# Modulation rows in a fixed order: all products, then three row turns, then the transpositions

## The chip, the cores and the metric

The kernel runs on one core of a Trainium2 chip. The metric is the device time of one execution in microseconds (us). The core has five engines that run beside each other, each with its own queue in order: TensorE (PE, with weight loads shown apart as PEld), VectorE (DVE), ScalarE (ACT), GpSimd (POOL) and SyncE (SP), which issues most transfers. An engine waits for another only at a semaphore, and whatever stands behind a waiting instruction in the same queue waits with it.

## The reference

One block of a diffusion transformer over 2048 tokens of width 1024, with 256 context tokens. What matters here is its beginning:

```python
mod_x = (jax.nn.silu(c) @ w_mod[layer] + b_mod[layer])[:, None, :]
mod_c = jax.nn.silu(c_ctx) @ w_mod[layer] + b_mod[layer]
sh1, sc1, g1, sh2, sc2, g2 = jnp.split(mod_x, 6, axis=-1)
csh1, csc1, cg1, csh2, csc2, cg2 = jnp.split(mod_c, 6, axis=-1)
hx = _rmsnorm(x, norm1_g[layer]) * (1.0 + sc1) + sh1
hc = _rmsnorm(ctx, norm1_g[layer]) * (1.0 + csc1) + csh1
feats_x = _mixer_features(hx, w_in[layer], lb, (rows, cols))
```

Nothing of the token mixers can start before the shift `sh1` and the scale `sc1` are known: a vector of 1024 inputs times a 1024 x 2048 part of `w_mod`, for two vectors (`c` and `c_ctx`). Behind this come two mixers with four heads each, the output projection, and a convolutional feed-forward network.

## The kernel before

The 2048 tokens are worked in four groups of 512; the last group (3) comes first. `heads` is the driver of the first two thirds of the time. It begins with the weights of head 0 (`items`: `w_z`, `w_q`, `w_vg`, each weight turned into pairs of 16-bit numbers by a cast on ACT, line 703 or 760, and a subtraction on DVE, line 704 or 761, with a few sums of quarters between them, lines 548 to 557), and with the modulation.

The 2048 columns of the modulation that are needed first are worked as four quarters of 512 columns, in the order 2, 3, 0, 1. Each quarter takes these steps:

- `mod_first` (line 292): eight PE products of 512 columns, each with one of eight 128-row pieces of the quarter's weights (`wm`), into four squares of 32 rows of one PSUM bank, `mod_ps`. Two banks of this kind (tag `sc`) are there.
- `mod_rows`: a copy of that bank to SBUF, the row `modrow` (line 256 on ACT, or 258 on DVE for quarter 0); four small PE products that turn the row into columns, the "row turn" (`modt_ps`, line 263); and one DVE addition of the bias into `modT` (line 266).

Quarter 2 is done early, with both kernels alike. Then `norm_rows` normalises the first 512 tokens (`x3`, whose eight pieces of 128 x 512 are shown as `hc` and `x`): eight squares with sums, all on ACT (line 398), a sum on DVE (402), six small POOL instructions for the reciprocal root (`rstd`, lines 71 to 76), and the scaling of the eight pieces by it, half on DVE (409) and half on ACT (407). `modulation` forms from `modT` the scale `modu` and the sums `modq` (DVE, lines 355 to 369), which go through one PE product (`allsum`) and five tiny DVE instructions to a power of two, `p2s`. `first_blocks` transposes the normalised tokens on PE (`tp`, line 416), applies scale and shift (`ftmp`, lines 460 on ACT and 458 on DVE), and casts to pairs of 16-bit numbers (`hx`, lines 435 on ACT and 436 on DVE) with `p2s`; then the first product of a head can run.

The order in each engine's queue is set by a scheduler that builds the program in the order of the code and moves instructions by its own estimates; `issue_after(x)` in the code keeps an instruction behind `x` in that order. It is no wait on the chip. Waits come from the data alone, buffers that are used again among them.

Of the kernel before, what the change touches and what calls it, by code (L numbers as in the profile page):

```python
# [9 lines left out]
F32 = mybir.dt.float32  # L10
# [4 lines left out]
AF = mybir.ActivationFunctionType  # L15
# [3 lines left out]
P = 128  # L19
# [13 lines left out]
KL = 3  # L33
# [21 lines left out]
class Kern:  # L55
# [191 lines left out]


    def mod_rows(self, rows, nr, j4):


        nc = self.nc
        if nr == 2:
            rs = self.mp.tile([P, 512], F32, tag="Kl", bufs=KL, name="modrow")
            if j4:
                nc.scalar.copy(rs, rows)
            else:
                nc.vector.tensor_copy(rs, rows)
            rows = rs
        ps = self.ps("tu", [P, 4, 2], "modt_ps")  # L260
        for j in range(4):
            sel = self.sel if nr == 2 else self.ones
            self.moded = nc.tensor.matmul(ps[:, j, :nr], rows[:, j * P:(j + 1) * P], sel, start=True, stop=True, skip_group_check=True)
        o = self.modT[:, :nr, 4 * j4:4 * j4 + 4].rearrange("p d j -> p j d")
        bm = view(self.sv, V_BM + 4 * j4, [[1, 4], [0, nr]])
        nc.vector.tensor_tensor(o, ps[:, :, :nr], bm, ALU.add)
# [19 lines left out]
    def mod_first(self, j4):  # L286

        nc = self.nc
        ps = self.ps("sc", [P, 512], "mod_ps")
        for k, w in enumerate(self.wm[j4]):  # L290
            q = k % 4 * B
            nc.tensor.matmul(ps[q:q + B], self.silb[:, k], w, start=k < 4, stop=k >= 4, skip_group_check=True)
        return ps
# [91 lines left out]

    def norm_rows(self, g, xn, behind=None):

# [5 lines left out]
        for i in range(nt):  # L393
            for h in range(2):
                on_act = True
                with self.tc.issue_after(behind[on_act].ins) if behind else nullcontext():
# [5 lines left out]
        nc.vector.tensor_tensor(ssq[:, :nt], sq[:, :nt, 0], sq[:, :nt, 1], ALU.add)  # L402
        r = self.rstd(self.mp, ssq[:, :nt], nt, D)
        for i in range(nt):
            for h in range(2):
                if h:
                    nc.scalar.activation(xn[i][h], xn[i][h], AF.Copy, scale=r[:, i:i + 1])
                else:
                    nc.vector.tensor_scalar(xn[i][h], xn[i][h], r[:, i:i + 1], None, ALU.mult)
        return xn  # L410
# [8 lines left out]
    def first_blocks(self, g, xn, places, bank, plain=False):  # L419
# [26 lines left out]
        for k0 in (0, 2):  # L446
            f = [places[k0 + r]() for r in range(2)]
            units = [(slice(k0, k0 + 2), f)] if len(f[0]) == len(f[1]) == 1 else [(slice(k0 + i, k0 + i + 1), []) for i in range(2)]
            for i in range(2):
                k = k0 + i  # L450
                at = [(v[0][:, i] if len(v) == 1 else v[i])[:, :2 * n] for v in f]
                for r in range(2):
                    kk = k + 4 * r
                    with self.tc.issue_after(self.moded.ins) if plain and k + r > 1 else nullcontext():
                        tp = self.transposed(xn, kk, bank)
# [241 lines left out]
    def pair_blocks(self, raws, W, s, neg, eng):  # L697

        nc = self.nc

        def emit(m, v):
            sc = neg if m == 3 else s
            nc.scalar.activation(W[m][:, 0], v, AF.Copy, scale=sc)  # L703
            nc.vector.scalar_tensor_tensor(W[m][:, 1], v, sc, W[m][:, 0], ALU.mult, ALU.subtract)  # L704
        blocks = [r[:, 4 * c:4 * c + 4] for r in raws for c in range(2)]
        yield from self.left_blocks(blocks, emit, eng.tensor_tensor)
# [332 lines left out]
    def heads(self):  # L1039
# [6 lines left out]
        self.small_vectors()  # L1046
        self.mod_rows(r2, 2, 2)
        self.lower_bounds()
        for _, comp in items[4:]:
            comp()  # L1050
        self.norm_rows(NG - 1, self.x3)
        self.mod_rows(self.mod_first(3), 2, 3)
        rows = [self.mod_first(j) for j in range(2)]
        for j in range(2):
            self.mod_rows(rows[j], 2, j)
        place = [self.gate_tile() for _ in range(4)]
# [941 lines left out]
```

## Time and profile before

| | |
|---|---|
| median of 3 runs | 2597.32 us (2592.52 to 2599.94) |
| profiled execution | 2600.73 us, span 2599.0 us |
| mean granted TensorE clock | 0.989 |
| PE busy | 2500.6 us (96% of the span) |
| DVE, ACT, POOL busy | 1895.5, 1351.0, 385.4 us |
| DMA | 402.36 MB, 155 GB/s in the mean |

The span is the time from the first to the last instruction of the profiled execution; 1.7 us of its device time lie around it. In a row of the timeline stand the start, the time to the end of the last of the instructions that it merges, the engine, the line, what is written and read, the number, and in brackets how long the engine had been idle and what ended that. Of the matrix products of this kind of 32-bit data each one shows as two instructions in the trace.

### The profile page before, as it was taken

What the parts mean: (1) busy time and instruction counts of PE and PEld (TensorE: products, weight loads), DVE (VectorE), ACT (ScalarE), POOL (GpSimd) and SP (SyncE); (2) the same over time, 40 slices, a digit from 0 to 9 for tenths busy, and PEclk for the clock granted to TensorE, in tenths of its full rate; (3) what the DMA queues carried; (4) which work ended last, traced back from release to release, by engine and by line L of the source; (5) the groups of instructions that cost most, each with busy time, mean ns of one, the idle gap of its engine ahead of it and who ended that gap; (6) DMA issues with size and microseconds to landing.
All of it is one profiled execution on the core that took longest, in us unless ns stands there. A gap on an engine that the chain in (4) does not pass through costs nothing.

```text
span 2599.0 us, 56245 instructions
## 1 busy us (share of the span) xinstructions
PE 2500.6 (96%) x22761; PEld 1647.9 (63%) x22761; DVE 1895.5 (73%) x4304; ACT 1351.0 (52%) x2879; POOL 385.4 (15%) x377
## 2 busy tenths in 40 slices
PE   5899998999999999999999999999999999999998
PEld 3788887889899999895544444444444444444443
DVE  6798586776878777785659777888888887223766
ACT  7886466564655454553647555556655554211221
POOL 1100000000000000001232343434443442000000
PEclk8999999999999999999999999999999999999999
DMA  8334342442558667794421332233233326544552
GB/s 308 113 135 132 119 147 83 139 152 67 180 164 284 214 214 253 246 332 148 167 82 48 124 112 99 101 111 114 102 106 110 122 90 246 197 173 154 211 213 83
DMA packets 144789, 402.36 MB, mean 155 GB/s; under 512 B 16144, under 2 KB 16372, under 8 KB 139921
## 3 DMA queue, kind: packets, MB, share of 16 engines
q1 hardware_dynamic: 134976, 381.81, 42.0%
q10 hardware_dynamic: 9248, 16.79, 2.0%
q8 instruction: 178, 2.92, 0.5%
q14 instruction: 83, 0.67, 0.1%
q0 software_dynamic: 304, 0.17, 0.0%
HBM read 302.77 MB, written 95.94 MB: 153 GB/s over the span
## 4 chain that ended last, share of the span: by engine, by line
PE 72%; DVE 11%; issue 6%; ACT 5%; DMA 5%; POOL 1%; SPq 0%; ACTq 0%; DVEq 0%; POOLq 0%
PE pa L101 8%; PE pa L102 8%; PE pa L103 8%; PE pd L102 5%; PE pd L101 5%; PE pd L103 5%; PE pc L101 3%; PE pc L103 3%; PE pc L102 3%; PE pb L101 2%; PE pb L102 2%; PE pb L103 2%; DMA raw<-in_w_in_dram 2%; PE opp L101 2%; PE opp L103 2%
## 5 line engine op out<-in xcount | busy, mean ns | idle before, releaser
L101 PE MATMUL pa<-feat,w 128*128 128x512 f16 x704 | 265.5, 382 | 7.2 <-DVE tb L638 4.1
L103 PE MATMUL pa<-feat,w 128*128 128x512 f16 x704 | 268.5, 382 | 1.3 <-DVE w L704 1.3
L102 PE MATMUL pa<-feat,w 128*128 128x512 f16 x704 | 268.4, 381 | 0.0
L102 PE MATMUL pd<-wd,actl 128*128 128x512 f16 x616 | 233.3, 379 | 0.0
L103 PE MATMUL pd<-wd,actl 128*128 128x512 f16 x616 | 233.3, 379 | 0.0
L101 PE MATMUL pd<-wd,actl 128*128 128x512 f16 x616 | 232.6, 379 | 0.0
L103 PEld LDWEIGHTS <-w 128*128 128x128 f16 x1232 | 120.8, 98 | 150.3 <-DVE w L704 4.3
L102 PEld LDWEIGHTS <-w 128*128 128x128 f16 x1232 | 120.8, 98 | 149.4 <-issue 10.9
L101 PEld LDWEIGHTS <-w 128*128 128x128 f16 x1232 | 120.8, 98 | 142.0 <-issue 3.1
L102 PEld LDWEIGHTS <-hx 128*128 128x128 f16 x1824 | 178.7, 98 | 6.3 <-issue 4.2
L101 PEld LDWEIGHTS <-hx 128*128 128x128 f16 x1824 | 179.0, 98 | 2.4 <-DVE qs L690 0.3
L103 PEld LDWEIGHTS <-hx 128*128 128x128 f16 x1824 | 178.8, 98 | 1.3 <-issue 0.4
L1474 POOL TENSOR_TENSOR ssq<-ssq 128x1 f32<-128x1 f32 x16 | 6.7, 417 | 1136.1 <-ACT junk L1469 1136.1
L1719 ACT ACTIVATE st<-act,modT 128x512 f16<-128x512 f32 x154 | 107.3, 717 | 113.0 <-DVE act L1709 61.5
L1720 DVE SCALAR_TENSOR_TENSOR st<-act,modT,st 128x512 f16<-128x512 f32 x154 | 143.9, 967 | 29.0 <-ACT st L1719 28.6
L101 PE MATMUL pa<-w_vg,hx 128*128 128x128 f16 x800 | 141.6, 219 | 2.0 <-ACT ct L604 1.2
L102 PE MATMUL pa<-w_vg,hx 128*128 128x128 f16 x800 | 141.6, 219 | 0.3 <-DVE w_vg L704 0.3
L103 PE MATMUL pa<-w_vg,hx 128*128 128x128 f16 x800 | 141.5, 219 | 0.0
L103 PE MATMUL pc<-feat,w 128*128 128x512 f16 x352 | 133.3, 379 | 2.0 <-DVE w L704 2.0
L101 PE MATMUL pc<-feat,w 128*128 128x512 f16 x352 | 133.4, 379 | 0.3 <-ACT tb L604 0.3
L102 PE MATMUL pc<-feat,w 128*128 128x512 f16 x352 | 133.4, 379 | 0.0
L704 DVE SCALAR_TENSOR_TENSOR w<-wur,p2s,w 128x512 f16<-128x512 f32 x132 | 122.8, 938 | 6.0 <-ACT w L703 6.0
(553 smaller groups left out, 7305.1 us busy)
## 6 DMA issues: line engine op xcount, KB each, us to landing
hx<-hxd SPq DMA_DIRECT2D x212, 512.0 KB, 5.2
actd<-st SPq DMA_DIRECT2D x154, 256.0 KB, 2.0
actl<-actd SPq DMA_DIRECT2D x28, 1024.0 KB, 5.2
wur<-in_w_up_dram SPq DMA_DIRECT2D x44, 512.0 KB, 3.6
raw<-in_w_in_dram SPq DMA_DIRECT2D x36, 512.0 KB, 4.6
wm<-in_w_mod_dram SPq DMA_DIRECT2D x64, 256.0 KB, 4.2
hxd<-hx SPq DMA_DIRECT2D x28, 512.0 KB, 4.1
wdb<-in_w_down_dram SPq DMA_DIRECT2D x44, 256.0 KB, 3.8
```

Of the source, the lines that this page charges most:

```text
L101: mm(ps, lhs(0), rhs(0), start=start, stop=False, skip_group_check=True)
L102: mm(ps, lhs(0), rhs(1), start=False, stop=False, skip_group_check=True)
L103: mm(ps, lhs(1), rhs(0), start=False, stop=stop, skip_group_check=True)
L704: nc.vector.scalar_tensor_tensor(W[m][:, 1], v, sc, W[m][:, 0], ALU.mult, ALU.subtract)
L1474: nc.gpsimd.tensor_tensor(ssq[:, 0:1], ssq[:, 0:1], ssq[:, 1:2], ALU.add)
L1719: nc.scalar.activation(p[:, 0], v, AF.Copy, scale=s)
L1720: nc.vector.scalar_tensor_tensor(p[:, 1], v, s, p[:, 0], ALU.mult, ALU.subtract)
```

## The change

In `heads`, quarters 3, 0 and 1 are no longer worked one after another behind the norm. Their 24 products stand in one piece ahead of all row turns, the three row turns follow (each kept behind the last product), and the first transpositions, which had no such bound, are kept behind the last product too. `norm_rows` gets two arguments for the first tokens: its squares are kept behind the last cast of `w_vg`, and are shared, the even pieces on DVE and the odd ones on ACT; and between the squares and the scaling stand the products and row copies of quarters 3 (ACT) and 0 (DVE), with the scaling on each engine kept behind that engine's copy. The copy is a function of its own now, `mod_copy`.

```diff
--- before.py
+++ after.py
@@ -246,17 +246,15 @@
         nc.vector.tensor_scalar(self.omlb, self.lb, -1.0, 1.0, ALU.mult, ALU.add)
 
 
+    def mod_copy(self, rows, eng):
+
+        rs = self.mp.tile([P, 512], F32, tag="Kl", bufs=KL, name="modrow")
+        return rs, eng(rs, rows)
+
     def mod_rows(self, rows, nr, j4):
 
 
         nc = self.nc
-        if nr == 2:
-            rs = self.mp.tile([P, 512], F32, tag="Kl", bufs=KL, name="modrow")
-            if j4:
-                nc.scalar.copy(rs, rows)
-            else:
-                nc.vector.tensor_copy(rs, rows)
-            rows = rs
         ps = self.ps("tu", [P, 4, 2], "modt_ps")
         for j in range(4):
             sel = self.sel if nr == 2 else self.ones
@@ -289,7 +287,7 @@
         ps = self.ps("sc", [P, 512], "mod_ps")
         for k, w in enumerate(self.wm[j4]):
             q = k % 4 * B
-            nc.tensor.matmul(ps[q:q + B], self.silb[:, k], w, start=k < 4, stop=k >= 4, skip_group_check=True)
+            self.rowed = nc.tensor.matmul(ps[q:q + B], self.silb[:, k], w, start=k < 4, stop=k >= 4, skip_group_check=True)
         return ps
 
     def mod_later(self, j4):
@@ -383,7 +381,7 @@
                 self.nc.sync.dma_start(x[h], src[i * P:(i + 1) * P, h * 512:h * 512 + 512])
         return xn
 
-    def norm_rows(self, g, xn, behind=None):
+    def norm_rows(self, g, xn, behind=None, between=None):
 
         nc = self.nc
         nt = len(xn)
@@ -392,7 +390,7 @@
         sq = self.mp.tile([P, 4, 2], F32, tag="sq8", bufs=2, name="sq8")
         for i in range(nt):
             for h in range(2):
-                on_act = True
+                on_act = not between or h
                 with self.tc.issue_after(behind[on_act].ins) if behind else nullcontext():
                     if on_act:
                         nc.scalar.activation(self.junk, xn[i][h], AF.Square, accum_out=sq[:, i, h:h + 1])
@@ -401,12 +399,14 @@
         ssq = self.mp.tile([P, 4], F32, tag="ssq", bufs=2, name="ssq")
         nc.vector.tensor_tensor(ssq[:, :nt], sq[:, :nt, 0], sq[:, :nt, 1], ALU.add)
         r = self.rstd(self.mp, ssq[:, :nt], nt, D)
+        after = between() if between else None
         for i in range(nt):
             for h in range(2):
-                if h:
-                    nc.scalar.activation(xn[i][h], xn[i][h], AF.Copy, scale=r[:, i:i + 1])
-                else:
-                    nc.vector.tensor_scalar(xn[i][h], xn[i][h], r[:, i:i + 1], None, ALU.mult)
+                with self.tc.issue_after(after[h].ins) if after else nullcontext():
+                    if h:
+                        nc.scalar.activation(xn[i][h], xn[i][h], AF.Copy, scale=r[:, i:i + 1])
+                    else:
+                        nc.vector.tensor_scalar(xn[i][h], xn[i][h], r[:, i:i + 1], None, ALU.mult)
         return xn
 
     def transposed(self, xn, k, bank):
@@ -451,7 +451,7 @@
                 at = [(v[0][:, i] if len(v) == 1 else v[i])[:, :2 * n] for v in f]
                 for r in range(2):
                     kk = k + 4 * r
-                    with self.tc.issue_after(self.moded.ins) if plain and k + r > 1 else nullcontext():
+                    with self.tc.issue_after((self.moded if k + r > 1 else self.rowed).ins) if plain else nullcontext():
                         tp = self.transposed(xn, kk, bank)
                     ka, kb = (v[:, which, kk:kk + 1] for v in (A, B))
                     if r and (g is None or plain and i):
@@ -700,8 +700,8 @@
 
         def emit(m, v):
             sc = neg if m == 3 else s
-            nc.scalar.activation(W[m][:, 0], v, AF.Copy, scale=sc)
-            nc.vector.scalar_tensor_tensor(W[m][:, 1], v, sc, W[m][:, 0], ALU.mult, ALU.subtract)
+            cast = nc.scalar.activation(W[m][:, 0], v, AF.Copy, scale=sc)
+            self.laid = nc.vector.scalar_tensor_tensor(W[m][:, 1], v, sc, W[m][:, 0], ALU.mult, ALU.subtract), cast
         blocks = [r[:, 4 * c:4 * c + 4] for r in raws for c in range(2)]
         yield from self.left_blocks(blocks, emit, eng.tensor_tensor)
 
@@ -1044,15 +1044,21 @@
             comp()
         r2 = self.mod_first(2)
         self.small_vectors()
-        self.mod_rows(r2, 2, 2)
+        self.mod_rows(self.mod_copy(r2, nc.scalar.copy)[0], 2, 2)
         self.lower_bounds()
         for _, comp in items[4:]:
             comp()
-        self.norm_rows(NG - 1, self.x3)
-        self.mod_rows(self.mod_first(3), 2, 3)
-        rows = [self.mod_first(j) for j in range(2)]
-        for j in range(2):
-            self.mod_rows(rows[j], 2, j)
+        rows = {}
+
+        def columns():
+            for j, eng in ((3, nc.scalar.copy), (0, nc.vector.tensor_copy)):
+                rows[j] = self.mod_copy(self.mod_first(j), eng)
+            return rows[0][1], rows[3][1]
+        self.norm_rows(NG - 1, self.x3, self.laid, columns)
+        rows[1] = self.mod_copy(self.mod_first(1), nc.scalar.copy)
+        with self.tc.issue_after(self.rowed.ins):
+            for j in (3, 0, 1):
+                self.mod_rows(rows[j][0], 2, j)
         place = [self.gate_tile() for _ in range(4)]
         xc = self.load_rows(None, place)
         self.mod1 = self.modulation(self.ep, pool, view(self.sv, V_N1, [[0, 2], [1, 8]]), self.modT[:, :, 8:16],
```

What the scheduler makes of it differs in the first part of the program, to about the 115th microsecond of the trace of before, and in one short stretch a tenth of the way through PE's queue; behind and between these the queues of all engines hold the same instructions in the same order. SP's queue differs in one swap of two stores of `hx`; POOL's is the same. Names end in buffer numbers below. In the rows of ACT and DVE, the engine or DMA queue whose semaphore an instruction waits for stands after "waits".

PE's queue behind quarter 2, before; `mod_ps_423` is quarter 3, `mod_ps_440` quarter 0, `hc` with a number a piece of the first tokens:

```order
L292 MATMUL mod_ps_423<-wm_213,silb_175 32x512 x2
L416 MATMUL tp_509<-ident_160,hc0_153 128x128
L416 MATMUL tp_515<-ident_160,hc1_154 128x128
L416 MATMUL tp_521<-ident_160,hc0_153 128x128
L292 MATMUL mod_ps_423<-wm_215,silb_175 32x512 x2
L416 MATMUL tp_509<-ident_160,hc2_155 128x128
L416 MATMUL tp_521<-ident_160,hc2_155 128x128
L416 MATMUL tp_515<-ident_160,hc3_156 128x128
L416 MATMUL tp_509<-ident_160,hc4_157 128x128
L416 MATMUL tp_521<-ident_160,hc4_157 128x128
L416 MATMUL tp_515<-ident_160,hc5_158 128x128
L416 MATMUL tp_509<-ident_160,hc6_159 128x128
```

The fourth pair of products of quarter 3 stood behind three transpositions of normalised tokens, and quarter 0, with quarter 1 after it, behind eight more. The same place now, with `mod_ps_445` for quarter 1:

```order
L290 MATMUL mod_ps_445<-wm_225,silb_175 32x512 x2
L290 MATMUL mod_ps_445<-wm_227,silb_175 32x512 x2
L290 MATMUL mod_ps_445<-wm_229,silb_175 32x512 x2
L290 MATMUL mod_ps_445<-wm_231,silb_175 32x512 x2
L261 MATMUL modt_ps_456<-sel_177,modrow_424 128x2 x4
L261 MATMUL modt_ps_462<-sel_177,modrow_435 128x2 x4
L261 MATMUL modt_ps_468<-sel_177,modrow_454 128x2 x4
L416 MATMUL tp_509<-ident_160,hc0_153 128x128
L416 MATMUL tp_515<-ident_160,hc1_154 128x128
L416 MATMUL tp_521<-ident_160,hc0_153 128x128
L416 MATMUL tp_509<-ident_160,hc2_155 128x128
L416 MATMUL tp_521<-ident_160,hc2_155 128x128
```

All products and all row turns stand ahead of the first transposition.

ACT's queue around the squares (`junk`, `sq8`) of the first tokens, before:

```order
L398 ACTIVATE junk_394,sq8_395<-hc2_155 128x512 [waits DMAHW6_49,Activation_49]
L398 ACTIVATE junk_394,sq8_395<-hc3_156 128x512 [waits DMAHW7_49,Activation_49]
L398 ACTIVATE junk_394,sq8_395<-hc4_157 128x512 [waits DMAHW0_49,Activation_49]
L398 ACTIVATE junk_394,sq8_395<-hc5_158 128x512 [waits DMAHW1_49,Activation_49]
L398 ACTIVATE junk_394,sq8_395<-hc6_159 128x512 [waits DMAHW2_49,Activation_49]
L398 ACTIVATE junk_394,sq8_395<-x3_200 128x512 [waits DMAHW3_49,Activation_49]
L760 ACTIVATE w_q_329<-raw_194,p2s_337 128x512 [waits DVE_49]
L760 ACTIVATE w_q_330<-raw_194,p2s_337 128x512
L703 ACTIVATE w_vg_351<-raw_196,p2s_366 128x512 [waits DVE_49]
L703 ACTIVATE w_vg_352<-raw_196,p2s_366 128x512
L703 ACTIVATE w_vg_354<-raw_198,neg_372 128x512 [waits DVE_49]
L407 ACTIVATE hc1_154<-hc1_154,rs_y_407 128x512 [waits Pool_49]
```

The squares stood ahead of the casts of `w_q` and `w_vg`, and waited for ACT's own earlier square and their transfer alone. The same place now:

```order
L703 ACTIVATE w_vg_357<-raw_198,p2s_366 128x512 [waits DVE_49]
L703 ACTIVATE w_vg_356<-raw_196,p2s_366 128x512 [waits DVE_49]
L703 ACTIVATE w_vg_353<-raw_196,p2s_366 128x512 [waits DVE_49]
L396 ACTIVATE junk_394,sq8_395<-hc1_154 128x512 [waits DMAHW5_49,DVE_49]
L396 ACTIVATE junk_394,sq8_395<-hc3_156 128x512 [waits DMAHW7_49,DVE_49]
L396 ACTIVATE junk_394,sq8_395<-hc5_158 128x512 [waits DMAHW1_49,DVE_49]
L396 ACTIVATE junk_394,sq8_395<-x3_200 128x512 [waits DMAHW3_49,DVE_49]
L252 COPY modrow_454<-mod_ps_445 128x512 [waits DMAHW0_49,DMASW0_49,PE_49]
L407 ACTIVATE hc1_154<-hc1_154,rs_y_407 128x512 [waits Activation_49,Pool_49]
L407 ACTIVATE hc3_156<-hc3_156,rs_y_407 128x512 [waits Activation_49]
L407 ACTIVATE hc5_158<-hc5_158,rs_y_407 128x512 [waits Activation_49]
L407 ACTIVATE x3_200<-x3_200,rs_y_407 128x512 [waits Activation_49]
```

All casts stand ahead of the squares, only four squares are left, each waits for DVE, and the row copy of quarter 1 (`modrow_454`) stands between squares and scaling.

DVE's queue from the sum of the squares (`ssq`) to the scaling, before:

```order
L402 TENSOR_TENSOR ssq_404<-sq8_395 128x4 [waits Activation_49]
L116 TENSOR_SCALAR p2s_366<-p2i_365 128x1 [waits DVE_49]
L716 COPY dq_374<-p2i_365 128x1
L713 TENSOR_SCALAR neg_372<-p2s_366 128x1 [waits DVE_49]
L761 SCALAR_TENSOR_TENSOR w_q_329<-raw_194,p2s_337,w_q_329 128x512 [waits DMAHW1_49,Activation_49]
L761 SCALAR_TENSOR_TENSOR w_q_330<-raw_194,p2s_337,w_q_330 128x512 [waits Activation_49]
L704 SCALAR_TENSOR_TENSOR w_vg_351<-raw_196,p2s_366,w_vg_351 128x512 [waits DMAHW2_49,Activation_49]
L704 SCALAR_TENSOR_TENSOR w_vg_352<-raw_196,p2s_366,w_vg_352 128x512 [waits Activation_49]
L409 TENSOR_SCALAR hc0_153<-hc0_153,rs_y_407 128x512 [waits DMAHW4_49,Pool_49]
L409 TENSOR_SCALAR hc2_155<-hc2_155,rs_y_407 128x512 [waits DMAHW6_49]
L409 TENSOR_SCALAR hc4_157<-hc4_157,rs_y_407 128x512 [waits DMAHW0_49]
L409 TENSOR_SCALAR hc6_159<-hc6_159,rs_y_407 128x512 [waits DMAHW2_49]
```

The scaling stood ahead of most of the casts of `w_vg`. The same place now, behind the last cast:

```order
L704 SCALAR_TENSOR_TENSOR w_vg_353<-raw_196,p2s_366,w_vg_353 128x512 [waits Activation_49]
L398 SCALAR_TENSOR_TENSOR junk_394,sq8_395<-hc0_153 128x512 [waits DMAHW4_49]
L252 COPY modrow_435<-mod_ps_426 128x512 [waits DMASW3_49,DMASW4_49,DMASW2_49,DMASW5_49,DMASW1_49,PE_49]
L398 SCALAR_TENSOR_TENSOR junk_394,sq8_395<-hc2_155 128x512 [waits DMAHW6_49,Activation_49]
L398 SCALAR_TENSOR_TENSOR junk_394,sq8_395<-hc4_157 128x512 [waits DMAHW0_49,Activation_49]
L398 SCALAR_TENSOR_TENSOR junk_394,sq8_395<-hc6_159 128x512 [waits DMAHW2_49,Activation_49]
L400 TENSOR_TENSOR ssq_404<-sq8_395 128x4 [waits Activation_49]
L409 TENSOR_SCALAR hc0_153<-hc0_153,rs_y_407 128x512 [waits Pool_49]
L409 TENSOR_SCALAR hc2_155<-hc2_155,rs_y_407 128x512
L409 TENSOR_SCALAR hc4_157<-hc4_157,rs_y_407 128x512
L409 TENSOR_SCALAR hc6_159<-hc6_159,rs_y_407 128x512
L264 TENSOR_TENSOR modT_170<-modt_ps_456,sv_168 128x4x2 [waits PE_49]
```

Each of DVE's squares but the first waits for ACT, since all eight write the one tile `junk_394`; the row copy of quarter 0 (`modrow_435`) stands behind the first, and the additions into `modT` behind the scaling.

## The prediction

> **What bounds the kernel now.** I first read where PE, the engine with the most work, is not busy. The stretches of the span show for each the length, then PE's, PEld's, DVE's, ACT's and POOL's busy time, the granted clock, the DMA share and GB/s:
>
> ```profile
> 0.00:50.00 50.00, 28.06 (x141) 14.08 (x142) 26.63 (x83) 34.28 (x61) 8.26 (x21) 0.83 0.94 357
> ...
> 50.00:100.00 50.00, 40.25 (x449) 32.85 (x447) 41.30 (x83) 44.01 (x95) 4.88 (x12) 0.93 0.39 148
> ...
> 100.00:150.00 50.00, 43.19 (x576) 36.78 (x576) 44.68 (x122) 40.32 (x100) 3.17 (x6) 0.90 0.39 143
> ...
> 300.00:400.00 100.00, 98.02 (x1704) 87.87 (x1697) 79.10 (x209) 62.54 (x150) 0.00 (x0) 1.00 0.42 140
> ```
>
> PE is idle for 21.9 us of the first 50, 9.8 of the next, 6.8 of the next, and from then on it is nearly full. A change at the start is worth what it moves of the moment at which PE gets its work; once moved, PE carries the lead through. PE's own rows between 20 and 52 us show that moment:
>
> ```profile
> 24.91 3.55 PE L292 MATMUL mod_ps<-wm,silb 128*32 128x512 f32 x12
> ...
> 33.72 0.92 PE L416 MATMUL tp<-ident,hc 128*128 128x128 f32 x3 [5.26 <-DVE hc L409]
> ...
> 34.57 1.92 PE L292 MATMUL mod_ps<-wm,silb 128*32 128x512 f32 x4
> ...
> 44.10 1.91 PE L292 MATMUL mod_ps<-wm,silb 128*32 128x512 f32 x12
> ...
> 46.69 1.05 PE L263 MATMUL modt_ps<-sel,modrow 128*128 128x2 f32 x8 [0.69 <-ACT modrow L256]
> ...
> 48.71 0.35 PE L124 MATMUL allsum<-modq,ones 128*128 128x1 f32 x2
> ```
>
> PE waited 5.26 us for the first normalised piece, with products of quarter 3 queued behind it; the last products of quarter 1 ended at 46.0, the last row turn at 47.7, and the sum that gives `p2s` ran at 48.7. So before, the products were late because they stood behind the norm. Were their weights there? SP's row and the DMA row (one issue near 26.7 us; its last number is the time to landing):
>
> ```profile
> 17.11 9.95 SPq L277 DMA_DIRECT2D wm<-in_w_mod_dram  x12
> ...
> wm<-in_w_mod_dram SPq DMA_DIRECT2D x1, 512.0 KB, 10.6
> ```
>
> The last of the twelve pieces landed at about 26.7 + 10.6 = 37.3 us. This is the floor for the products, 8.7 us ahead of 46.0.
>
> **The change part by part.** The transfers do not move: SP's queue is the same up to a swap of two stores. PE has the same instructions. What must be followed is the norm, which now starts behind the casts. ACT and DVE before:
>
> ```profile
> 20.82 0.56 ACT L256 COPY modrow<-mod_ps 128x512 f32<-128x512 f32 x1
> ...
> 28.70 0.63 ACT L398 ACTIVATE junk<-x 128x512 f16<-128x512 f32 x1
> ...
> 29.23 0.19 ACT L398 ACTIVATION_READ_ACCUMULATOR junk<-x 128x1 f32 x1
> ...
> 29.32 1.32 ACT L760 ACTIVATE w_q<-raw,p2s 128x512 f16<-128x512 f32 x2
> ...
> 50.28 1.32 ACT L435 ACTIVATE hx<-ftmp,p2s 128x512 f16<-128x512 f32 x2
> ```
>
> ```profile
> 25.09 0.14 DVE L116 TENSOR_SCALAR p2s<-p2i 128x1 int32<-128x1 int32 x1
> ...
> 29.45 0.16 DVE L402 TENSOR_TENSOR ssq<-sq 128x4 f32<-128x4 f32 x1 [3.71 <-ACT junk L398]
> ...
> 30.06 1.41 DVE L761 SCALAR_TENSOR_TENSOR w_q<-raw,p2s,w_q 128x512 f16<-128x512 f32 x2 [0.20 <-ACT w_q L760]
> ...
> 31.39 1.41 DVE L704 SCALAR_TENSOR_TENSOR w_vg<-raw,p2s,w_vg 128x512 f16<-128x512 f32 x2
> ...
> 33.17 1.68 DVE L409 TENSOR_SCALAR hc<-hc,rs_y 128x512 f32<-128x512 f32 x4 [0.37 <-POOL rs_y L76]
> ...
> 34.76 0.75 DVE L704 SCALAR_TENSOR_TENSOR w_vg<-raw,neg,w_vg 128x512 f16<-128x512 f32 x1
> ...
> 40.60 0.74 DVE L704 SCALAR_TENSOR_TENSOR w_vg<-raw,p2s,w_vg 128x512 f16<-128x512 f32 x1
> ```
>
> *Casts.* Their scale `p2s` was ready at 25.2; ACT cast only from 29.32, behind eight squares. With the first square gone from ahead of the row copy of quarter 2 (20.82), that copy and what hangs on it come 0.6 us sooner, so casts begin at about 24.6 and DVE's part 0.74 later (29.32 to 30.06), at 25.4. DVE then has four casts at 0.67 (30.06 to 31.39 for two), to 28.1, and the stretch from 34.76 to 41.34, 6.6 us less 0.2 of a modulation row in it, to 34.5. ACT's casts lie beside this, and so does its row copy of quarter 3 (0.59 us).
>
> *Squares.* By the order they are no longer eight on one engine but a chain over two, DVE, ACT, DVE, ACT, each waiting for the one before. An ACT square with its sum takes 0.72 (28.70 to 29.42), a handover some 0.04 (29.42 to 29.45). A DVE square with a sum stands nowhere in the trace. The nearest row is a form with two 32-bit inputs:
>
> ```profile
> L1881 DVE SCALAR_TENSOR_TENSOR c<-c,rs_y,fgb 128x512 f32<-128x512 f32 x32 | 22.6, 747 | 0.3
> ```
>
> It gives 0.75 without a sum; with the 0.19 that ACT's read of its sum takes, 0.94 is the upper end, and back to back, at 0.67 a piece as the casts, the lower. I take 0.80, near the row. Four pairs of 0.80 + 0.72 + 0.08 are 6.4 us (5.9 to 7.0): done at 40.9. The row copy of quarter 0 (0.69) lies beside ACT's first square.
>
> *Root and scaling.* The sum and the handover to POOL take 0.25 (29.45 to 29.71): 41.15. POOL's six instructions have two prices:
>
> ```profile
> 29.71 0.18 POOL L71 TENSOR_SCALAR rs_v<-ssq 128x4 f32<-128x4 f32 x1 [22.09 <-DVE p2s L116]
> ...
> 32.94 0.20 POOL L76 TENSOR_TENSOR rs_y<-rs_y,rs_t 128x4 f32<-128x4 f32 x1
> ...
> 72.28 0.19 POOL L71 TENSOR_SCALAR rs_v<-ssq 128x4 f32<-128x4 f32 x1 [39.14 <-DVE ssq L402]
> ...
> 74.50 0.20 POOL L76 TENSOR_TENSOR rs_y<-rs_y,rs_t 128x4 f32<-128x4 f32 x1
> ```
>
> 3.4 us (29.71 to 33.14) beside DVE's casts, 2.4 (72.28 to 74.70) beside little DVE work. Now DVE waits for POOL and does nothing, so I take 2.4: 43.6. The Trainium skill, "SBUF — State Buffer", section "Who interferes with whom", says that a DVE instruction with two SBUF inputs contends with a GpSimd instruction that reads SBUF; the two rows agree, and by the rule the sum goes with 2.4, without it with 3.4 and ends 1.0 later. DVE's scaling (1.68) ends at 45.3; before, it began at 33.17. The norm is 10.4 us later than it was.
>
> *Products and turns.* The last pair of products is done 1.9 us (34.57, at the slow clock) after its landing: 39.2. Two turns of 1.05 follow, to 41.3. The third waits for quarter 1's row copy, which stands on ACT behind its last square: 40.9 + 0.6, and 1.05: 42.6. All that is covered by the norm; it would show if it took 2.7 us longer.
>
> *From there to the first cast of tokens.* The additions into `modT` stand on DVE behind the scaling, and then:
>
> ```profile
> 42.98 0.17 DVE L355 TENSOR_SCALAR modu<-modT 128x16 f32<-128x16 f32 x1
> ...
> 43.59 0.17 DVE L362 TENSOR_REDUCE modq<-modj 128x1 f32<-128x16 f32 x1
> ...
> 47.78 0.17 DVE L266 TENSOR_TENSOR modT<-modt_ps,sv 128x8 f32<-128x8 f32 x1 [3.41 <-PE modt_ps L263]
> ...
> 48.40 0.16 DVE L369 TENSOR_TENSOR modq<-modq 128x1 f32<-128x1 f32 x1
> ...
> 48.49 0.81 DVE L458 TENSOR_SCALAR ftmp<-tp,modu,modT 128x512 f32<-128x512 f32 x1
> ...
> 49.22 0.15 DVE L112 TENSOR_SCALAR p2t<-allsum 128x1 int32<-128x1 int32 x1
> ...
> 49.96 0.15 DVE L116 TENSOR_SCALAR p2s<-p2i 128x1 int32<-128x1 int32 x1
> ```
>
> Two stretches of 0.78 (42.98 to 43.76, 47.78 to 48.56) and two additions, 1.7 in all: 47.0. PE's sum with both handovers takes 0.5 (48.56 to 49.06): 47.5. Five tiny instructions take 0.9 (49.22 to 50.11), and the new order puts an evacuation (0.81, at 48.49 before and ahead of them) in front of the fifth: 49.15. ACT's first cast (50.28 before) starts there: **1.1 us earlier**. With the bounds of squares and root it is 1.6 earlier to 0.5 later.
>
> *Behind it.* ACT then has one evacuation more to do (about 0.7), which DVE, the busier engine in that stage, covers. Further on, ACT's queue in the second group of tokens is changed at a wait:
>
> ```profile
> 68.87 0.51 ACT L782 ACTIVATE FG<-cb,dq 128x256 f32<-128x256 f32 x1 [1.02 <-DVE cb L586]
> ```
>
> This gate activation waited 1.02 us with five squares of the second group ahead of it; now four stand ahead, and a second such activation moves in ahead of the last square. Their sum comes up to 0.7 + 0.5 = 1.2 us later against the rest, or no later where ACT has room. I take the middle, 0.6. The reordered stretch in head 1 lies where PE is nearly full and its work is the same: nothing. Sum: 1.1 - 0.6 = 0.5 us less. The profiled execution (2600.73) becomes 2600.2; it lies 3.4 above the median of 2597.32, so the median becomes **2596.8**.
>
> **The rivals.** (1) *The lead is larger.* If the squares ran side by side, the norm would be 3.2 us earlier, its scaling would end at 42.1, about level with the last turn (42.6): first cast some 4.2 earlier than before, net 3.6, 2593.7. For it: the two engines are free. Against it: the waits in the queues. A form of this that gains over 7.8 us needs the idle time of PE between 50 and 150 us to shrink too; I see nothing that does it.
>
> (2) *Slower: DVE's square is dear.* If a square with a sum took twice the row, 1.5 us, the chain would grow by 2.8 us, the first cast come 1.7 later than before, and with the 0.6 behind it the kernel would take 2.3 longer: 2599.6. It decides from 1.1 us a square on (0.80 + 1.1 / 4). For it: no row shows that instruction. Against it: the row of 0.747 with two 32-bit inputs. The Trainium skill, "Vector Engine (DVE) Microarchitecture Reference", section "7. Points that are easy to get wrong", says that this shape with two SBUF sources that are not bf16 halves its throughput. By that rule this rival would hold; the row does not show the halving where no sum is asked for.
>
> (3) *Nothing arrives.* From 50 to 150 us ACT and DVE are 81 to 89% busy, and if their total, and not the first cast, sets when PE is filled, the lead is lost: 2597.3.
>
> (4) *Slower by over 0.3%*: displaced waits like that at 68.87 in each of the four token groups and the context, over 1.5 us each: 2605 and more.
>
> **How the numbers follow.** A change under 0.3%, 7.8 us, can't be told from none here. Chances: the forecast (2595 to 2598.5) 0.50; (1) 0.13, and 0.06 for its form over 7.8 us; (2) 0.11; (3) 0.15; (4) 0.05. So faster 0.06, same 0.89, slower 0.05. The range takes in (1) and (2) and the scatter of a few runs, 2592.5 to 2599.9 before: 2591 to 2602.
>
> **What the profile after would show.** The casts of `w_q` from 24.6; squares alternating from 34.5 to 41 with no two at a time; POOL's root in 2.4 us near 41 to 43.6; PE's products in one piece, paced by landings and done by 39.2; `p2s` at about 49. The prediction is wrong if the squares overlap, if a DVE square is far from 0.8, if products end after 45, or if the wait at 68.87 grows by over 2 us.

## Result, and the profile after

The changed kernel takes 2592.59 us (median of 20 runs, 2587.74 to 2597.08) where the kernel before took 2596.79 beside it (20 runs, 2592.52 to 2600.65): a ratio of 0.9983, 95% interval 0.9976 to 0.9990, or 4.4 us less (2.6 to 6.2). Timed again among the experiments it had 0.9979 (0.9970 to 0.9988). The forecast was 0.5 us less. The sign holds, and the time lies within the stated range of 2591 to 2602, but not within the 2595 to 2598.5 of the forecast itself: most of the gain came from a place that the forecast had put at nothing.

The stretches of the span of after, columns as in those of before (PE was 28.06, 40.25, 43.19 and 98.02 there):

```profile
0.00:50.00 50.00, 31.12 (x143) 15.97 (x144) 29.90 (x98) 32.06 (x54) 7.25 (x21) 0.83 0.93 357
50.00:100.00 50.00, 40.58 (x458) 33.69 (x458) 42.75 (x81) 43.80 (x96) 4.24 (x12) 0.92 0.41 156
100.00:150.00 50.00, 43.46 (x605) 37.49 (x602) 43.67 (x121) 40.85 (x102) 3.17 (x6) 0.91 0.37 138
...
300.00:400.00 100.00, 97.76 (x1659) 87.33 (x1656) 77.75 (x204) 62.69 (x151) 0.00 (x0) 1.00 0.37 126
```

At the start of the program the chain to the first cast of tokens takes the forecast's steps in their order. PE's products run in one piece, paced by landings (first and last row), and are done at 38.2; then come the turns:

```profile
24.27 5.91 PE L290 MATMUL mod_ps<-wm,silb 128*32 128x512 f32 x24
...
37.12 1.05 PE L290 MATMUL mod_ps<-wm,silb 128*32 128x512 f32 x4 [0.26 <-DMA wm<-in_w_mod_dram]
38.10 1.95 PE L261 MATMUL modt_ps<-sel,modrow 128*128 128x2 f32 x16
40.63 1.42 PE L261 MATMUL modt_ps<-sel,modrow 128*128 128x2 f32 x8 [0.58 <-ACT modrow L252]
43.41 2.63 PE L416 MATMUL tp<-ident,hc 128*128 128x128 f32 x11 [1.36 <-DVE hc L409]
...
46.29 0.56 PE L124 MATMUL allsum<-modq,ones 128*128 128x1 f32 x2
```

DVE's squares, with ACT's between them:

```profile
34.20 0.68 DVE L398 SCALAR_TENSOR_TENSOR junk<-hc 128x512 f16<-128x512 f32 x1
34.81 0.08 DVE L398 DVE_READ_ACCUMULATOR junk<-hc 128x1 f32 x1
...
37.16 0.69 DVE L398 SCALAR_TENSOR_TENSOR junk<-hc 128x512 f16<-128x512 f32 x1 [0.79 <-ACT junk L396]
...
38.65 0.69 DVE L398 SCALAR_TENSOR_TENSOR junk<-hc 128x512 f16<-128x512 f32 x1 [0.79 <-ACT junk L396]
...
40.13 0.16 DVE L400 TENSOR_TENSOR ssq<-sq 128x4 f32<-128x4 f32 x1 [0.79 <-ACT junk L396]
42.87 1.67 DVE L409 TENSOR_SCALAR hc<-hc,rs_y 128x512 f32<-128x512 f32 x4 [2.57 <-POOL rs_y L76]
...
45.98 0.16 DVE L367 TENSOR_TENSOR modq<-modq 128x1 f32<-128x1 f32 x1
46.88 0.16 DVE L112 TENSOR_SCALAR p2t<-allsum 128x1 int32<-128x1 int32 x1 [0.74 <-PE allsum L124]
...
48.57 0.14 DVE L116 TENSOR_SCALAR p2s<-p2i 128x1 int32<-128x1 int32 x1
```

ACT's first casts of weights, one of its squares, and its last evacuation (`ftmp`, transposed tokens read out of PSUM) ahead of the first cast of tokens:

```profile
24.63 1.34 ACT L760 ACTIVATE w_q<-raw,p2s 128x512 f16<-128x512 f32 x2 [0.83 <-DVE p2s L116]
...
37.89 0.63 ACT L396 ACTIVATE junk<-hc 128x512 f16<-128x512 f32 x1 [0.77 <-DVE junk L398]
...
48.42 0.78 ACT L460 ACTIVATE ftmp<-tp,modT,modu 128x512 f32<-128x512 f32 x1 [0.66 <-PE tp L416]
49.10 1.32 ACT L435 ACTIVATE hx<-ftmp,p2s 128x512 f16<-128x512 f32 x2
```

Each engine waits 0.77 to 0.79 us for the other between two squares, and a pair costs 1.49 us. The first cast of tokens is at 49.10, 1.18 ahead of before.

**Where the time went.** For each place the ACT, DVE and POOL rows of two executions can be paired by name and order; the lead is the median by which a row starts earlier than in the execution of before that the prediction used. "Cast" is the first cast of tokens:

| kernel | cast | lead at 110-120 | 140-150 | 240-260 | 300-350 | ratio of times (95%) |
|---|---|---|---|---|---|---|
| before, again | 50.50 | -0.3 | -0.3 | -0.5 | 0.5 | - |
| after | 49.10 | 2.8 | 1.3 | 2.0 | 5.0 | 0.9983 (0.9976-0.9990) |
| after, again | 48.98 | 2.8 | 1.4 | 1.7 | 4.7 | 0.9979 (0.9970-0.9988) |

Behind 350 us the leads of two executions of one program differ by 3 us and more (before, again: 2.9 at 1200 to 1300, 0.0 at the end; after and after, again: 3.7 and 9.9 at the end), so only what stands above is read. In these two executions of after the lead of the start is 1.3 to 2.0 us; 3.0 us come at 255 to 285 us, in the stretch that the change only reordered. The size of this step hangs on the execution of before: "before, again" gains 0.9 there by itself, and against it the step is 2.1 in both executions of after. There, in before, on ACT:

```profile
263.19 1.06 ACT L750 ACTIVATE w_z<-raw 128x1024 f16<-128x1024 f32 x1 [2.27 <-DMA raw<-in_w_in_dram]
...
264.25 0.57 ACT L934 COPY ou<-uf 128x512 f32<-128x512 f32 x1
266.56 1.06 ACT L750 ACTIVATE w_z<-raw 128x1024 f16<-128x1024 f32 x1 [1.74 <-DMA raw<-in_w_in_dram]
...
267.61 0.35 ACT L604 COPY ct<-pa 128x256 f32<-128x256 f32 x1
267.86 0.37 ACT L604 COPY cb<-pc 128x256 f32<-128x256 f32 x1
```

Two square sums of the next head's weights (L750) wait for a DMA at the head of ACT's queue; a copy that DVE needs (L934), and two copies that free PSUM for PE (L604), stand behind them. DVE and PE, of before:

```profile
264.85 0.35 DVE L965 SCALAR_TENSOR_TENSOR ou<-cs,T,ou 128x128 f32<-128x128 f32 x1 [2.88 <-ACT ou L934]
```

```profile
265.51 0.49 PE L944 MATMUL op<-KTt,Q 128*128 128x128 f32 x2 [1.38 <-DVE KTt L946]
...
268.01 0.22 PE L101 MATMUL pa<-w_vg,hx 128*128 128x128 f16 x1 [0.60 <-ACT ct L604]
```

These 1.38 + 0.60 us are PE's only waits of more than 0.2 us from 256 to 290 us. Its stretches in before:

```profile
260.00:265.00 5.00, 4.13 (x59) 3.86 (x56) 1.99 (x5) 2.48 (x5) 0.00 (x0) 1.00 0.69 206
265.00:270.00 5.00, 3.89 (x50) 3.71 (x51) 4.03 (x12) 2.17 (x5) 0.00 (x0) 1.00 0.56 217
```

In after the copies are ahead:

```profile
257.83 0.58 ACT L934 COPY ou<-uf 128x512 f32<-128x512 f32 x1
...
262.45 1.06 ACT L750 ACTIVATE w_z<-raw 128x1024 f16<-128x1024 f32 x1 [1.76 <-DMA raw<-in_w_in_dram]
...
263.51 0.35 ACT L604 COPY ct<-pa 128x256 f32<-128x256 f32 x1
263.76 0.37 ACT L604 COPY cb<-pc 128x256 f32<-128x256 f32 x1
265.02 1.06 ACT L750 ACTIVATE w_z<-raw 128x1024 f16<-128x1024 f32 x1 [0.88 <-DMA raw<-in_w_in_dram]
```

ACT waits here too, but nobody waits for ACT; PE is busy 5.00 of 5 us in each of the three stretches from 255 on:

```profile
255.00:260.00 5.00, 5.00 (x70) 4.46 (x69) 5.00 (x11) 3.94 (x7) 0.00 (x0) 1.00 0.02 5
260.00:265.00 5.00, 5.00 (x70) 4.93 (x68) 3.46 (x11) 2.05 (x5) 0.00 (x0) 1.00 0.83 239
265.00:270.00 5.00, 5.00 (x83) 4.90 (x82) 2.14 (x4) 3.38 (x12) 0.00 (x0) 1.00 0.81 265
```

### The profile page after: what moved, and what is told of

It reads as the page before. It is cut to its first block, busy times and chain, and to the rows that moved or that the text cites. A ratio compares the mean times of both kernels' runs of the same rounds, so it can differ in the third digit from the quotient of the medians.

```text
span 2595.3 us, 56248 instructions
## 1 busy us (share of the span) xinstructions
PE 2504.1 (96%) x22761; PEld 1651.8 (64%) x22761; DVE 1897.2 (73%) x4312; ACT 1347.0 (52%) x2871; POOL 383.5 (15%) x377
## 4 chain that ended last, share of the span: by engine, by line
PE 74%; DVE 11%; issue 5%; DMA 5%; ACT 4%; POOL 1%; SPq 0%; ACTq 0%; DVEq 0%; POOLq 0%
PE pa L101 8%; PE pa L102 8%; PE pa L103 8%; PE pd L102 5%; PE pd L101 5%; PE pd L103 5%; PE pc L101 4%; PE pc L102 4%; PE pc L103 4%; PE pb L101 3%; PE pb L102 2%; PE pb L103 2%; DMA raw<-in_w_in_dram 2%; PE opp L101 2%; PE opp L103 2%
## 5 line engine op out<-in xcount | busy, mean ns | idle before, releaser
L101 PE MATMUL pa<-hx,w_z 128*128 128x256 f16 x464 | 126.9, 273 | 1.2 <-DVE K L646 1.1
```

The lines of the kernel that those rows point to most:

```text
L101: mm(ps, lhs(0), rhs(0), start=start, stop=False, skip_group_check=True)
```

## Experiments

To keep all else in place, most of these kernels add edges that set only the order of issue: a list of an engine's instructions, each to be issued behind the one before it. The core of it, shortened:

```python
for i in rows_of_engine:
    if last is not None:
        tc.add_manual_dep(i, last.name, NoSync, reason="in_row")
    last = i
```

One added import moves the line numbers of e1 and e2 by one. The leads are those of the table above:

| kernel | cast | 110-120 | 140-150 | 240-260 | 300-350 | ratio (95%) |
|---|---|---|---|---|---|---|
| e1 before, new stretch | 50.91 | -0.6 | -0.7 | -0.3 | 2.6 | 0.9988 (0.9980-0.9997) |
| e2 after, old stretch | 49.47 | 2.4 | 0.8 | 0.0 | 0.2 | 0.9998 (0.9989-1.0007) |
| e3 squares side by side | 48.25 | 3.6 | 3.6 | 3.8 | 6.6 | 0.9974 (0.9965-0.9982) |
| e4 norm early | 48.46 | 2.9 | 2.9 | 3.2 | 6.1 | 0.9977 (0.9968-0.9986) |
| e5 squares and copy | 45.61 | 6.1 | 6.1 | 6.3 | 6.7 | 0.9969 (0.9960-0.9979) |
| e6 PSUM copies ahead | 50.88 | 0.5 | -0.7 | -0.4 | 0.4 | 1.0000 (0.9990-1.0009) |
| e7 ou copy ahead | 50.72 | 0.7 | 0.7 | 0.9 | 1.4 | 0.9998 (0.9990-1.0006) |
| e8 both ahead | 50.55 | 0.9 | 0.9 | 1.1 | 2.9 | 0.9991 (0.9982-1.0000) |
| e9 e5, later squares moved | 46.46 | 4.7 | 4.7 | 4.5 | 7.6 | 0.9986 (0.9977-0.9995) |
| e10 squares on ACT | 48.69 | 3.7 | 2.4 | 2.3 | 5.4 | 0.9992 (0.9983-1.0001) |

**The two parts apart.** e1 is before with the stretch's rows of ACT (38), DVE (39) and PE (279) in the order of after; e2 is after with those rows in the order of before.

```diff
+ROWS = {"ACT": "... KTt x2, w_vg x2, ou<-uf, w_vg, ct_4246<-pa, w_z_5017, ct_3968, cb_3969, w_z_5018 ...",   # e1
+        "DVE": ..., "PE": ...}
+in_row(nc, tc)
```

> The kernel before in all but one stretch (some 255 to 285 us): ScalarE, VectorE and TensorE issue their rows there in the order of the changed kernel, in which copies out of PSUM (L604) stand ahead of the square sums of the next head's weights (L750) that wait for a DMA. The modulation is that of before. Theory (the stretch is worth 3.1 us by itself, the start of the program 1.3): no lead over before up to 250 us, a lead of about 3.1 us from 285 us on, and 2596.8 - 3.1 = 2593.7 us. Rival (all of the gain comes from the start of the program, the step at 280 us is scatter of one execution): 2596.8 us, no step.

> The changed kernel with the stretch of some 255 to 285 us put back into the order of before; the modulation is the changed one. Theory: the lead of 1.3 to 1.9 us that the start gives stays through 285 us without a step, and the time is 2596.8 - 1.3 = 2595.5 us (to 2594.9 if the drift to 1.9 before the stretch is lasting). Rival (the step is scatter): 2592.6 us, as the changed kernel.

e1 has no lead before the stretch and a step of 3.0 in it (2.1 against before, again); its time is 0.9988. e2 has no step in it, and 0.9998, with an interval that leaves out after's 0.9983. The rival falls: the stretch alone brings 2.1 to 3.0 us in the trace and 3.1 (0.8 to 5.2) in time. The theory's other half, that the start keeps a lead of 1.3 to 1.9 us, did not hold in e2: its lead was 0.8 at 140 to 150 us and 0.0 at 240 to 260. In time, what the start alone brings can't be told from nothing: e2 gives 0.5 us with an interval of 2.3 either way. "After, again" had the step a second time:

> The changed kernel once more. If the step of the stretch at 255 to 285 us is of the program, this execution has it again, 3.0 us within 0.3; if the loss at 120 us is scatter, it is absent or elsewhere. Time: 0.9983 of before, within 0.001.

> The kernel before once more, for a second profiled execution of it. If the drift of 1 to 2 us that the comparisons show after 300 us, and the loss of 1.4 us at 120 us in the changed kernel, are scatter of one execution (the granted clock falls at other places in each), the two executions of before differ by as much, at places of their own.

The step is 3.0 again (1.7 to 4.7). The two executions of before differ by 0.3 to 0.5 ahead of the stretch, by 0.9 within it and by up to 3 behind it. Within the stretch, the second square's DMA wait was 0.86 instead of 1.74 in before, again, and PE did not wait for the copies behind it:

```profile
265.97 1.06 ACT L750 ACTIVATE w_z<-raw 128x1024 f16<-128x1024 f32 x1 [0.86 <-DMA raw<-in_w_in_dram]
```

On the loss at 120 us I was probably wrong to think of scatter alone, though the executions are few. It stands in all three with after's start (after, again, e2), and in one of six with before's (e6). The stretch in after, in after again and in before:

```profile
120.00:125.00 5.00, 5.00 (x45) 4.85 (x45) 3.57 (x13) 3.42 (x7) 0.00 (x0) 0.69 0.00 0
```

```profile
120.00:125.00 5.00, 5.00 (x46) 4.89 (x45) 3.49 (x12) 3.46 (x7) 0.00 (x0) 0.71 0.00 0
```

```profile
120.00:125.00 5.00, 3.98 (x40) 3.11 (x41) 4.44 (x18) 4.85 (x9) 0.00 (x0) 1.00 0.00 0
```

The granted clock is 0.69 and 0.71 of full there, and 0.66 in e2 and e6; e10, which loses 1.2 us too, had 0.83 from 115 to 125 us. It is 1.00 there in before and in all the others, and none of these loses. 5 us at 0.7 would cost 1.5 us, an estimate from the clock of these rows; 1.2 to 1.6 are lost.

**Which wait in the stretch.** e6, e7 and e8 are before with one row, another row, and both moved on ACT; on DVE, PE and SP no row moves.

```diff
 w_z_5017<-raw_4715          # first square sum       e7, e8: -ou below, +ou here above it
 ou_4001<-uf_3996
-w_z_5018<-raw_4717          # second square sum      e6, e8
 ct_3968<-pa_3970
 cb_3969<-pc_4065
+w_z_5018<-raw_4717
```

> The kernel before with one row moved: ScalarE's second square sum of the next head's weights (L750, it waited 1.74 us for its DMA at 266.56) stands behind the two copies out of PSUM (L604) that came after it. Theory (each of two waits in ScalarE's queue held TensorE by itself; this one held it 0.60 us): the copies run at about 264.9, TensorE's wait of 0.60 us for them goes, the wait of 1.38 us for VectorE's KTt stays: 0.6 us of lead after 270 us. Rival (the step of the stretch came from TensorE's and VectorE's order, not from ScalarE's waits): no lead.

> The kernel before with one row moved: ScalarE's copy ou<-uf (L934) stands ahead of the first square sum (L750, it waited 2.27 us for its DMA) instead of behind it. Theory: VectorE's wait of 2.88 us for this copy and TensorE's wait of 1.38 us for VectorE's KTt go, but the two copies out of PSUM still stand behind the second square sum, whose DMA lands at the same time (about 266.5), so that TensorE waits for them 0.60 + 1.38 = 2.0 us instead: no lead after 270 us. Rival (the first wait alone made the loss): 1.4 us of lead.

> The kernel before with both moves: the copy ou<-uf ahead of the first square sum, and the second square sum behind the two copies out of PSUM. Theory (ScalarE's queue is the cause, and the two waits hide one another): TensorE is busy without a gap from 260 to 270 us, 1.4 + 0.6 = 2.0 us of lead after 270 us, two thirds of the 3.0 us that the whole of the stretch's new order gave, 2594.8 where before has 2596.8. Rival (TensorE's order is the cause): no lead.

PE's waits in e6, in e7, and in e8 the stretches instead, as no wait is left:

```profile
265.84 0.49 PE L944 MATMUL op<-KTt,Q 128*128 128x128 f32 x2 [1.29 <-DVE KTt L946]
```

```profile
266.59 0.22 PE L101 MATMUL pa<-w_vg,hx 128*128 128x128 f16 x1 [1.83 <-ACT ct L604]
```

```profile
260.00:265.00 5.00, 5.00 (x67) 4.99 (x66) 3.88 (x12) 2.47 (x6) 0.00 (x0) 1.00 0.81 248
265.00:270.00 5.00, 5.00 (x83) 4.91 (x83) 2.37 (x6) 3.37 (x13) 0.00 (x0) 1.00 0.92 302
```

In e7 the first wait goes and the second grows from 0.60 to 1.83. In e8, which differs from e7 by one moved row, both are gone, and the step is 1.8 instead of 0.5. So PE's two waits come from ACT's queue, and moving the first row alone only brings out the second wait. e6 settles nothing: its wait of 0.60 is gone, but so it is in before, again, where nothing was moved, and its step (0.9) is that of before, again. In time e6 and e7 equal before, and e8 has 0.9991 with an interval that ends at 1.0000.

Of the whole step of 3.0, the two moves in e8 give 1.8 (0.9 of 2.1 against before, again). What the rest goes with is not shown. DVE's and PE's new order is one candidate. The clock is another: in e8's execution it was 0.91 from 250 to 255 us and 0.75 from 255 to 260, against 1.00 in before and e7, and the lead of PE's rows fell there from 1.1 to 0.3 us.

**The start.** e3 gives the squares two scratch rows. In e3, e4, e5 and e10 all that follows the first tokens is held in the order of after.

```diff
-self.junk = self.mp.tile([P, 512], F16, tag="qf3", ...)
+self.junk = self.mp.tile([P, 2, 512], F16, tag="qf3", ...)
-... self.junk, ...
+... self.junk[:, 0], ...      # ACT;  [:, 1] on DVE
```

> The changed kernel with two scratch rows, so that VectorE's and ScalarE's squares of the first rows don't overwrite one another's; everything from the first block of tokens on is issued in the order of the changed kernel. Theory (the two engines alternated for the scratch tile alone, 1.49 us a pair; side by side four squares of 0.77 us on ScalarE end about 37.6 instead of 40.1): sum of squares at 37.6, scaling ends 42, first cast of tokens about 46.8 instead of 49.1, and the lead of 2.3 us passes on to the end as that of the change did: 2590.3 us. Rival (another thing is late next, the modulation's turns at 42.6 or a load): first cast at 48.5 or later and 2592 to 2593 us.

The sum of squares stands at 37.46, as expected, but the first cast only at 48.25, as the rival has it: ACT's last row copy now stood behind four scalings. Its row in e3:

```profile
42.66 0.56 ACT L252 COPY modrow<-mod_ps 128x512 f32<-128x512 f32 x1
```

Still its lead is 1.6 to 2.3 above after's from 140 us on, as the clock did not fall at 120 in this execution, and the time is 0.9974. e5 puts that copy first:

```diff
-for j, eng in ((3, nc.scalar.copy), (0, nc.vector.tensor_copy)):
+for j, eng in ((3, nc.scalar.copy), (0, nc.vector.tensor_copy), (1, nc.scalar.copy)):
     rows[j] = self.mod_copy(self.mod_first(j), eng)
-return rows[0][1], rows[3][1]
+return rows[0][1], rows[1][1]
```

> The kernel of the squares side by side, and the last quarter's copy of product rows on ScalarE ahead of its four scalings instead of behind them; from the first projection on in the order of the changed kernel. Theory (with the squares ended at 37.5 the first cast waited for this copy, which ended at 43.2 behind scalings that wait for the root until 40.2, while its products were done at 39.0): copy 39.0 to 39.6, last turn by 42.5, scales of the modulation by 45, first cast at 45.5 to 46 instead of 48.25, and the lead over before grows by the same 2.3 to 2.7 us up to the end: about 9 us below before. Rival (the loads or the norm of the next block of rows are late next): first cast at 46, but a lead at 130 us no larger than the 3.6 us of the squares alone, and 6 to 7 us below before.

```profile
39.04 0.59 ACT L252 COPY modrow<-mod_ps 128x512 f32<-128x512 f32 x1 [3.15 <-PE mod_ps L290]
...
45.61 0.72 ACT L435 ACTIVATE hx<-ftmp,p2s 128x512 f16<-128x512 f32 x1
```

The copy is at 39.04 and the first cast at 45.61, as expected, and 6.1 us of lead hold from 110 to 260 us. At 0.9969 it has the lowest ratio of all, 8.1 us below before, though its interval overlaps those of e3 and e4. In the stretch it gained only 0.4: in its execution the granted clock was 0.50 from 250 to 255 us, where after had 1.00.

e4 leaves squares and scaling where before had them and changes only the products; e10 is e5 with all squares on ACT.

```diff
-self.norm_rows(NG - 1, self.x3, self.laid, columns)     # e4
+self.norm_rows(NG - 1, self.x3)
+columns()
-on_act = not between or h                               # e10
+on_act = True
```

> The changed kernel's order of products, turns and transpositions, but the squares and scaling of the first rows where the kernel before had them: all eight squares on ScalarE, ahead of the casts of the weights; from the first block of tokens on in the order of the changed kernel. Theory (in before the first cast waited for the last quarter's product, turn and copy, no longer for the rows): ScalarE's casts of weights move back by eight squares of 0.77 us (6.2 us), the copies of product rows stand behind them at about 40.5, turns and columns end at 43.5, first cast at about 47.5, 1.6 us ahead of the changed kernel: 2591.0 us. Rival (the casts of the weights, pushed back, hold the copies so long that nothing is won): first cast 49 to 50.5, 2592.6 to 2594 us.

> The kernel of squares and copy with all eight squares of the first rows on ScalarE and none on VectorE; from the first projection on in the order of the changed kernel. Theory (with one scratch tile the changed kernel's two engines took 6.0 us for eight squares, no less than ScalarE alone takes for eight of 0.76 us, and they began later, behind VectorE's casts): squares 32.9 to 39.0, sum at 39.2 against 40.1 in the changed kernel, root 41.7, scaling to 44.4, first cast between 47 and 48 against 49.1, so that the changed kernel's share of squares for VectorE bought nothing; about 0.9975 of before. Rival (VectorE's share is needed: ScalarE becomes the bound of the start): first cast at 49 or later and 0.9983 or more.

e4's first cast is at 48.46, between theory and rival, and 0.6 ahead of after: the late norm is not needed for the gain. Its root ran beside DVE's casts and took 3.4 us (29.51 to 32.94). e10 had its sum at 38.66, ahead of after's 40.13 as the theory has it, but the first cast at 48.69: ACT did five evacuations ahead of it and the modulation's sum stood behind ten transpositions. The time, 0.9992, is no better than after's; between theory and rival nothing is decided by it.

**The rule at other places.** e9 is e5 with three later square sums behind copies; there the scheduler was free.

```diff
+for i, last in (("w_q_5690", "cb_5806"), ("w_q_8576", "A_7962"), ("w_vg_8603", "Kl_8906")):
+    behind(i, last)
```

> The kernel of squares and copy, and in the next two heads three square sums of weights that wait 2 to 4 us for their DMA (at 342, 503 and 531 us, where TensorE idled 1.0, 1.9 and 1.5 us behind them) put behind the copies out of PSUM and operand copies that came after them, as in the stretch; what the scheduler moves with them is left to it. Theory (the rule of the stretch holds at the other places): TensorE's three waits go, up to 4.4 us of lead more by 560 us, and some 3 us below the kernel of squares and copy, 0.9958 of before. Rival (what the square sums deliver, the scales of the next weights, is late next, or the scheduler's other moves cost as much): no gain over 0.9969.

The rival holds: 0.9986, more than e5. PE's waits at 342 and 503 us are gone. The one at 531 is only shorter, 0.92 us instead of the 1.62 of e5: there PE waits for what the square sum itself delivers, so that moving copies ahead of it could not remove it. Between some 450 and 560 us e9 gains 1.8 us on e5; but between 300 and 450 it had lost 2.3, where the scheduler reordered rows of ACT, DVE and PE around the first of the three. Its first cast was 0.85 later than e5's with the same order up to there, which is scatter.

## Why the forecast was right, and where it was not

| step | forecast | measured |
|---|---|---|
| casts begin; DVE's casts end | 24.6; 34.5 | 24.63; 34.28 |
| a pair of squares; the sum of squares | 1.60; 40.9 | 1.49; 40.1 |
| POOL's root | 2.4 | 2.4 |
| products, last turn | 39.2, 42.6 | 38.2, 42.05 |
| first cast of tokens | 49.15 | 49.10 |
| given back at 50 to 120 us | 0.6 | -1.6, then 1.4 at 120 |
| the reordered stretch | 0 | -3.0 (-2.1 against before, again) |

The time of 2592.59 lies outside the forecast's own 2595 to 2598.5 and next to the 2593.7 of rival (1), whose mechanism did not take place. That it lies within the stated range is owed to the width of the range, not to the sum.

The chain to the first cast was right in its steps, and that 49.10 meets 49.15 is partly luck, since two errors cancel. The squares were 0.8 sooner. From the end of `modq` (46.14) to the cast it took 2.96 instead of 2.15. The forecast's 0.5 for PE's sum "with both handovers" left the second handover out: before's own rows give 0.66, from 48.56 to DVE's next instruction at 49.22, and after has 0.74. Then `p2s` was ready at 48.71, but ACT stood until 49.10 in an evacuation (48.42) that had waited 0.66 us for a transposition, with PE's granted clock at 0.50 to 0.52 from 42 to 48 us. Over all executions the first cast lies at 50.28 to 50.91 with before's start (six) and at 48.98 to 49.47 with after's (three), 1.5 us apart in the mean.

DVE's square with a sum was the unknown of rival (2): 0.68 us and 0.08 for reading the sum, near the row of 0.747 and below the 0.80 taken. The Trainium skill, "Vector Engine (DVE) Microarchitecture Reference", section "7. Points that are easy to get wrong", would have it at half the throughput; the measurement decides against that here. The Trainium skill's rule in "SBUF — State Buffer", section "Who interferes with whom", on which the prediction drew, agrees with the trace: POOL's root took 2.4 us with DVE idle in after (40.40 to 42.83) and 3.4 beside DVE's casts in e4.

Rival (1), squares side by side, put the first cast 4.2 us ahead of before. The queues forbade it, as said; where the scratch tile allows it the cast is 2.0 ahead (e3), and 4.7 with the row copy moved (e5).

Two steps failed. "Their sum comes up to 0.7 + 0.5 = 1.2 us later against the rest": the gate activation did not come later. It stands at 66.29, 2.58 ahead of before's 68.87, and waits for nothing:

```profile
66.29 0.49 ACT L782 ACTIVATE FG<-cb,dq 128x256 f32<-128x256 f32 x1
```

PE's granted clock from 60 to 65 us was 1.00 where before had 0.74 (before again 0.78), and the same projections ended sooner. The forecast had taken the clock of one execution as given. The change is not needed for the higher clock: e6, e7 and e8 have before's order up to there, and had it too. Before and e6:

```profile
60.00:65.00 5.00, 3.41 (x18) 2.14 (x17) 5.00 (x9) 4.80 (x10) 0.00 (x0) 0.74 0.38 155
```

```profile
60.00:65.00 5.00, 3.44 (x30) 2.63 (x28) 5.00 (x9) 4.22 (x8) 0.00 (x0) 1.00 0.45 185
```

```profile
68.37 0.49 ACT L782 ACTIVATE FG<-cb,dq 128x256 f32<-128x256 f32 x1
```

In these three the gate activation waits for nothing either, and between the first cast and 110 us they gain 1.1 us of lead, where before, again and e1 gain nothing and after gains 1.6. So some 1.1 us of the 1.6 go with the clock, and the other 0.4 to 0.5 with the new order. The clock fell there in three of six executions with before's start and in none of eight with a changed start; whether the change keeps it up is not shown. Of the 1.6 us won so, 1.4 are lost at 120 us.

And: "The reordered stretch in head 1 lies where PE is nearly full and its work is the same: nothing." This is the large error. Where PE is nearly full, a wait of PE can't be made good behind it. The work was the same, but ACT's queue was not, and in it two instructions waited for a DMA ahead of copies on which PE and DVE depended. The trace of before showed both waits of ACT, and the chain of waits has 2% of the span at "DMA raw<-in_w_in_dram". I had asked what each moved row costs, not who stands behind a waiting one.

## What to carry to other kernels

An instruction that waits for a DMA holds all that stands behind it in its engine's queue, however little the engine has to do: look whether what frees PSUM or feeds a full engine can stand ahead of it, and where two such waits follow one another, move both, since moving one may only bring out the other (e7). It is no rule to apply blindly: at three more places it gained nothing in sum, and at one of them PE waited for the waiting instruction's own result (e9). When a scheduler reorders a place that the edit does not touch, read the waits there before calling it nothing. The two engines that wrote one scratch tile took turns here; with a second row of scratch the sum of squares came at 37.46 instead of 40.13 (e3). And the size of a step between two executions is uncertain by as much as two executions of one kernel differ there: profile the kernel before twice, too.

## What was unexpected of the hardware

- The granted clock fell at different places, in executions of one order of instructions too: 0.74 to 0.80 at 60 to 65 us in three of six executions with before's start and 1.00 in the other three; 0.66 to 0.71 at 120 to 125 us in three of three with after's start and one of six with before's, 1.00 there in e3 and e5; and 0.50 at 250 to 255 in the one execution of e5. The time lost by it over the span, an estimate from the clock of its stretches of 10 us, was 23 to 35 us in 14 executions. What sets it off was not found.
- A sum's read cost DVE 0.08 us and ACT 0.19 us, so that a square with its sum takes 0.70 on DVE (35.67 to 36.37 in after) and 0.72 on ACT (34.92 to 35.64).
